# A 31-tap depthwise convolution as float32 diagonal products in four column groups of TensorE

## The chip, the cores and the metric

The kernel runs on one core of a Trainium2 chip, in one launch. The metric is the device time of that core in microseconds, the median over several runs. The engines are TensorE (PE in the profile, its weight loads PEld), VectorE (DVE), ScalarE (ACT), GpSimd (POOL) and SyncE (SP), which issues most of the DMAs.

## What is computed

Two transformer blocks work on 512 tokens of width 1024, all in float32. The first block has a parallel mixer, an attention to a memory of 256 tokens and a gated feed-forward part; the second has four gated feed-forward parts, a pooling mixer and a latent attention. The change touches the parallel mixer alone:

```python
def parallel_mixer(h, w_in, conv_dw, conv_dw_b, conv_ln_g, conv_ln_b, q_norm_g, k_norm_g, w_out, tabs):
    z = jnp.einsum("bsd,dc->bsc", h, w_in)
    ...
    a = a_val * jax.nn.sigmoid(a_gate)          # 512 channels, 512 tokens
    a = dwconv_centred(a, conv_dw, conv_dw_b)   # 31 taps a channel, zeros at both ends
    a = layernorm(a, conv_ln_g, conv_ln_b)      # over the 512 channels of a token
    a = jax.nn.silu(a)
    ...
    att = gqa_blocked(q, k, v)                  # 8 query heads of 64, 2 key heads
    mixed = jnp.concatenate([a, att], axis=-1)
    return jnp.einsum("bsc,cd->bsd", mixed, w_out)
```

## The kernel before

Activations lie with channels in the 128 partitions and the 512 tokens along the row. A float32 product is made exact by splitting both factors into a high part (type fp32r, made by a cast) and the low rest: `mm3` (L165) issues three TensorE matmuls, high x high, high x low and low x high. Weights come in units of 128 x 1024 words. `fetch` (L127) loads a unit into one of three `raw` buffers through SP's queue, and `cook` (L132) makes its high part on ScalarE (L138) and its low part on VectorE or GpSimd (L140); of the cooked parts there are three buffers each, too. `wshare` says how many of four units get their low part from GpSimd: all four in the mixer's input projection and in the memory's key and value projections (`W_IN, W_KV = 4, 4`), none in the output projection.

The mixer (L561) multiplies with `w_in` in 14 output tiles (`linear`, L172). Their order is `ORDER`: pairs of a gate and a value tile, which give the four channel tiles of the convolution, with k, v and four tiles of q between and behind them. `ev_gate` (L580) and `ev_val` (L597) turn a pair into the conv's input `at`, twice the gated value; half the conv's weights make up for it. Then come eight heads of attention, one head ahead: `scores` and `attend` (L682, L693), and after each head two units of the memory's projections (`mem_kv`, L464). The output projection multiplies attention's half first, then the conv's half.

The convolution of a channel tile is shared by two engines. `conv_pe` (L522) does six of the 31 taps on TensorE, as products with diagonal 128 x 128 matrices `dg` that GpSimd makes from the weights (L530), in exact parts: 18 matmuls for a tile into a PSUM tile `cps`, with shifts of whole pairs of words. `conv_taps` (L542) does the other taps: one on ScalarE (L548, with the bias), 24 on VectorE, each one instruction that multiplies a shifted row by its weight and adds (L556), and at last the sum with `cps` (L559). The taps are a generator that the mixer steps by hand: six taps behind each tile of the input projection, up to 30 before the attention and eight behind each head (`STEP_IN`, `STEP_PRE`, `STEP_HEAD`). `conv_norm` (L737) is the layernorm over the channels, also in steps, behind heads 3, 6 and 7; its mean is one float32 product of 512 columns (L745).

A float32 operand that isn't split goes to TensorE as it is. So do the sums of squares of the norms (`sums`, L202): float32 products with 32 output columns, one for each block of 128 tokens, whose four results go to the four groups of 32 partitions of one PSUM tile:

```python
for j in range(nb):
    self.nc.tensor.matmul(ps[32 * j:32 * j + 32, o:o + P], sel,
                          sq[:, j * P:(j + 1) * P], start=..., stop=...)
```

The order of the instructions on each engine is set when the kernel is built: a scheduler takes the program in its written order as priority, and lets ready instructions pass waiting ones by a model of their times. On the chip each queue then runs in that fixed order. Tiles come from pools with a fixed number of buffers; `xs` has 16 (the split input of the projection, then the attention's probabilities), `cv` nine (the conv), `pt` two in PSUM.

Of the kernel before, what the change touches and what calls it, by code (L numbers as in the profile page):

```python
# [26 lines left out]
# order of the taps' offsets: the even ones from the middle, then the odd ones  # L27
TAPS = sorted(range(-(KTAPS // 2), KTAPS // 2 + 1), key=lambda d: (d % 2, abs(d), d))
# [5 lines left out]
_VECS = [  # L34
    ("g_mix", 8), ("conv_w", 4 * KTAPS), ("conv_b", 4), ("cln_g", 4), ("cln_b", 4),
# [25 lines left out]
class Kern:  # L61
# [41 lines left out]
    # -- small access helpers --  # L103
# [7 lines left out]

    def t(self, tag="t", dt=F32, w=S, name="t"):
        return self.pools[tag].tile([P, w], dt, name=name, tag=tag)
# [7 lines left out]
    def turn(self, out, src):  # L121
        """Transpose by PE, which moves float32 words unchanged."""
        n = src.shape[0]
        return self.nc.tensor.transpose(out, src, self.ident[:n, :n])  # L124

    # -- weights: DRAM -> raw -> exact parts hi + lo --
# [17 lines left out]
    def lo_on_pool(self):  # L144
        """Share of the units (in fourths) whose low part GpSimd makes."""
        self.wturn = (self.wturn + 1) % 4
        return self.wturn < self.wshare
# [9 lines left out]
    def load_tile(self, w, nt, nk):  # L157
        """Stationary tiles of output tile nt: list over k of (hi, lo) [P, P]."""
        res = []
        for k0 in range(0, nk, 8):  # L160
            n = min(8, nk - k0)
            res += self.tiles(self.load_unit(w[nt, :, k0 * P:(k0 + n) * P], n * P), n)
        return res

    def mm3(self, ps, w, x, start, stop):  # L165
        """ps += w.T @ x with w, x each given as exact (hi, lo) parts."""
        mm = self.nc.tensor.matmul
        mm(ps, w[0], x[0], start=start, stop=False)  # L168
        mm(ps, w[0], x[1], start=False, stop=False)  # L169
        self.mmi = mm(ps, w[1], x[0], start=False, stop=stop)  # L170
# [10 lines left out]
    # -- split an fp32 tile (SBUF or PSUM), optionally scaled per partition --  # L181
# [31 lines left out]
    def columns(self, sm, dim, eps=0.0, w=1):  # L213
        """sm / dim + eps in columns [P, block, w], in PSUM."""
# [8 lines left out]
    def newton(self, v, n):  # L223
        """rsqrt of v [P, n] on the vector engine."""
# [14 lines left out]
    def rstd(self, sqs, dim, nb=4):  # L239
        """rsqrt(mean + eps) in columns from squares [P, nb * P], summed over the list."""  # L240
# [27 lines left out]
    def bcast_ps(self, R, nb=4, w=1):  # L268
        """Columns to rows of all partitions (row r of w in its share of them), exact float32."""
# [14 lines left out]
    def expand(self, R, w, tag="t"):  # L284
        """Columns -> [32 * block + r, tokens], zero outside the block, as exact parts."""
# [13 lines left out]
    def spread(self, X, r, tag="mi"):  # L299
        """Row r of every block, on all partitions."""  # L300
# [6 lines left out]
    # -- residual stream --  # L307
# [5 lines left out]
    def gather(self, sqs, sq, last, w=S):  # L313
        """Sum of squares so far: at most two tiles, the last one kept apart."""
# [6 lines left out]
    def pre(self, gname, dve_squares=(), tag2="xs"):  # L321
        """Gain times x as exact parts, and the reciprocal rms in quadrant form."""
# [14 lines left out]
    def post_collect(self, gname, tag="xs"):  # L337
        """Evacuation of a stage's output that a norm follows; pre() of the next stage adds it."""
# [10 lines left out]
    def settle(self):  # L349
        """Generator: adds the pending normed output to x, a tile a step."""  # L350
# [24 lines left out]
    def warm(self, ps, n):  # L375
        """Keeps PE's clock up while it waits: n products that nobody reads, right behind the
        last matmul."""
# [13 lines left out]
    # ------------------------------------------------------------------  # L391
    def softmax_rows(self, ps, w, f, tag):
        """softmax over ps[:, :w] * f (f: [P, 1], positive)."""
# [12 lines left out]
    def rope(self, src, g, gs, cos, sin):  # L406
        """Rotary embedding along the partitions (pairs 16 apart), gains g, gs folded in."""
# [11 lines left out]
    def stack(self, src, r, tag, on_pool=False):  # L419
        """Exact parts of the 64 rows src[64 r:], one in each half of a tile."""  # L420
# [8 lines left out]
    # -- block 1: parallel mixer --  # L429
    def mem_load(self, i):  # L430
        """Two 256-token tiles of the memory side by side."""
# [16 lines left out]
    def mem_prep(self):  # L448
        """Gain times memory as exact parts."""
# [14 lines left out]
    def mem_kv(self):  # L464
        """Generator: key and value projections of the memory, a weight unit a step."""
# [37 lines left out]
    NPE = 6  # L503
    PE_AT = 0
    CP_TAG = "pt"
    STEP_IN = 6
    KV_HEAD = 2
    STEP_PRE = 30
    STEP_HEAD = 8
    KT_TAG = "pr"  # L510
    PT_TAG = "t"
    CN_AT = (3, 6, 7)
    CN_AF = (0, 0, 1)
    ORDER = (0, 1, 8, 2, 3, 9, 4, 5, 10, 6, 7, 11, 12, 13)
    W_IN, W_KV, W_OUT, W_MEM = 4, 4, 0, 1

    def tap(self, n):
        """Output and input ranges of tap n."""
        d = TAPS[n]
        return (slice(0, S - d), slice(d, S)) if d >= 0 else (slice(-d, S), slice(0, S + d))  # L520

    def conv_pe(self, i, at):  # L522
        """The taps of channel tile i that run on PE, as products with diagonal matrices."""
        nc = self.nc
        ah, al = self.split(at, None, "cv", name="ah")
        ps = self.ps(self.CP_TAG, "cps")
        for n0 in range(0, self.NPE, 2):
            c = 2 * (i * KTAPS + n0)
            dg = self.t("pr", F32R, name="dg")
            nc.gpsimd.tensor_tensor(  # L530
                out=dg.rearrange("p (n t) -> p n t", n=4),
                in0=self.ident.unsqueeze(1).to_broadcast([P, 4, P]),
                in1=self.cws[:, c:c + 4].bitcast(F32).unsqueeze(2).to_broadcast([P, 4, P]),
                op=ALU.mult)
            for n in range(2):
                o, s = self.tap(n0 + n)
                hi, lo = dg[:, 2 * n * P:(2 * n + 1) * P], dg[:, (2 * n + 1) * P:(2 * n + 2) * P]
                self.mm3(ps[:, o], (hi, lo), (ah[:, s], al[:, s]), n0 + n == 0,
                         n0 + n == self.NPE - 1)
        return ps  # L540

    def conv_taps(self, i, at, acc):  # L542
        """Generator: the other taps of channel tile i, on DVE."""
        nc = self.nc
        w = lambda n: self.cwh[:, i * KTAPS + n:i * KTAPS + n + 1]
        first = KTAPS // 2
        o, sl = self.tap(first)
        nc.scalar.activation(acc[:, o], at[:, sl], AF.Identity, scale=w(first),  # L548
                             bias=self.v("conv_b", i))
        nc.gpsimd.tensor_copy(acc[:, :1], self.v("conv_b", i))  # L550
        ps = None
        for m, n in enumerate(n for n in range(self.NPE, KTAPS) if n != first):
            if m == self.PE_AT:
                ps = self.conv_pe(i, at)
            o, s = self.tap(n)
            nc.vector.scalar_tensor_tensor(out=acc[:, o], in0=at[:, s], scalar=w(n),  # L556
                                           in1=acc[:, o], op0=ALU.mult, op1=ALU.add)
            yield
        nc.vector.tensor_tensor(out=acc, in0=ps, in1=acc, op=ALU.add)  # L559

    def mixer(self):  # L561
        nc = self.nc
        a = self.a
        self.cwh = self.t("tb", name="cwh")[:, :4 * KTAPS]
        ws0 = {0: self.tiles(self.cook(self.raw0, UNIT, 4), 8)}
        xs, R1 = self.pre("g_mix", (1, 3, 5))
        nc.gpsimd.tensor_scalar(out=self.cwh, in0=self.v("conv_w", 0, 4 * KTAPS), scalar1=0.5,
                                scalar2=1.0, op0=ALU.mult, op1=ALU.mult)
        self.cws = self.t("tb", F32R, name="cws")[:, :8 * KTAPS]
        c2 = self.cws.rearrange("p (k two) -> p k two", two=2)  # L570
        nc.scalar.copy(c2[:, :, 0], self.cwh)
        nc.gpsimd.tensor_tensor(out=c2[:, :, 1], in0=self.cwh, in1=c2[:, :, 0].bitcast(F32),
                                op=ALU.subtract)
# [3 lines left out]
        # n-tiles: 0..7 (gate_i, val_i), 8 k, 9 v, 10..13 q pairs  # L577
        ats = []
# [7 lines left out]
        convs = []  # L586
        accs = []

        def step(n):
            while n and convs:  # L590
                try:
                    next(convs[0])
                    n -= 1
                except StopIteration:
                    convs.pop(0)

        def ev_val(nt, ps):  # L597
            i = nt // 2
            at = self.t("cv", name="at")
            acc0 = self.t("cv", name="acc0")  # L600
            nc.vector.tensor_tensor(out=at, in0=ps, in1=rb, op=ALU.mult)
            nc.vector.scalar_tensor_tensor(out=at, in0=st["g"], scalar=1.0, in1=at, op0=ALU.add,
                                           op1=ALU.mult)
            accs.append(acc0)
            convs.append(self.conv_taps(i, at, acc0))
# [3 lines left out]
        def ev_k(nt, ps):  # L609
# [6 lines left out]
            # both halves of a tile hold the same kv head  # L616
# [776 lines left out]
```

## Time and profile before

| | |
|---|---|
| median of 3 runs | 2589.59 us (2588.21 to 2589.89) |
| profiled execution | 2588.3 us from its first to its last instruction |
| TensorE busy | 2496.1 us (96%) |
| VectorE busy | 1385.5 us (54%) |
| ScalarE, GpSimd busy | 919.1 us (36%), 521.8 us (20%) |
| TensorE's mean granted clock | 0.985 of full |
| the mixer | about the first 322 us |

The profile is of one execution. A row of a group gives line, engine, operation, the tiles written and read, the shapes and the count, then busy time and mean duration, then the idle time of the engine just before and what ended it. A TensorE record lasts longer than the distance to the next one, since matmuls are pipelined: the distance between starts is the cost. The mean granted clock is taken over the whole span.

### The profile page before, as it was taken

Reading aid. Unit: us, or ns where it says so; the run is one execution under the profiler, and the core shown is the slowest. Engines: PE = TensorE matmul, PEld = TensorE weight load, DVE = VectorE, ACT = ScalarE, POOL = GpSimd, SP = SyncE. Lnnn points to the kernel's source line nnn. Section 1 sums busy time; section 2 is a strip of 40 time slices with the busy share of each in tenths; the row PEclk is TensorE's granted clock in tenths of the full one; section 3 lists DMA queues with packets and bytes.
Section 4 is the critical chain, followed back from the end, with each engine's and each line's share of the span. In section 5 each row is a group of like instructions: output and inputs, shape, how many; then the busy total and the mean of one; then the engine's idle time right before and its main releaser. Section 6 shows DMA issues by size and latency. Waiting matters only on the chain.

```text
span 2588.3 us, 29365 instructions
## 1 busy us (share of the span) xinstructions
PE 2496.1 (96%) x11668; PEld 2037.2 (79%) x11668; DVE 1385.5 (54%) x1877; ACT 919.1 (36%) x1332; POOL 521.8 (20%) x417
## 2 busy tenths in 40 slices
PE   7879989899999899999999999999999999999999
PEld 6667768688888688888888888888887778888887
DVE  7997563686632645533655543555433576555522
ACT  3336534354422333322422322323222455422221
POOL 4575232311100311101211100111000144111100
PEclk9889999999999999999999999999999999999999
DMA  4211211133333222234232333223332210333232
GB/s 163 66 67 49 90 57 58 64 98 98 96 95 97 69 94 96 95 98 132 74 98 98 97 98 96 97 95 95 98 98 88 78 62 19 104 98 97 92 107 79
DMA packets 68201, 229.80 MB, mean 89 GB/s; under 512 B 7456, under 2 KB 9632, under 8 KB 68064
## 3 DMA queue, kind: packets, MB, share of 16 engines
q1 hardware_dynamic: 66688, 225.35, 27.1%
q0 software_dynamic: 1232, 2.36, 0.3%
q8 instruction: 91, 1.49, 0.2%
q14 instruction: 46, 0.38, 0.0%
q10 hardware_dynamic: 144, 0.23, 0.0%
HBM read 225.80 MB, written 2.10 MB: 88 GB/s over the span
## 4 chain that ended last, share of the span: by engine, by line
PE 86%; DVE 4%; ACT 1%; issue 0%; ACTq 0%
PE ps L169 26%; PE ps L168 26%; PE ps L170 26%; DVE x L369 1%; DVE xl L190 1%; PE wo L168 1%; PE wo L169 1%; PE wo L170 1%; PE pt L124 1%; PE po L169 0%; PE bc L274 0%; PE po L168 0%; PE po L170 0%; PE sc L168 0%; DVE wlo L140 0%
## 5 line engine op out<-in xcount | busy, mean ns | idle before, releaser
L138 ACT CAST whi<-raw 128x1024 fp32r<-128x1024 f32 (+2 forms) x432 | 440.5, 1021 | 1217.7 <-PE ps L169 767.5
L140 DVE TENSOR_TENSOR wlo<-raw,whi 128x1024 fp32r<-128x1024 f32 (+2 forms) x400 | 559.3, 1400 | 492.6 <-ACT whi L138 487.5
L169 PE MATMUL ps<-xl,whi 128*128 128x512 f32 x2008 | 789.8, 394 | 18.6 <-DVE xl L190 18.5
L168 PE MATMUL ps<-xh,whi 128*128 128x512 f32 x2008 | 784.9, 393 | 15.0 <-ACT xh L189 14.7
L170 PE MATMUL ps<-xh,wlo 128*128 128x512 f32 x2008 | 786.6, 392 | 0.0
L169 PEld LDWEIGHTS ps<-xl,whi 128*128 128x128 f32 x2008 | 380.5, 189 | 104.6 <-DVE xl L190 25.0
L168 PEld LDWEIGHTS ps<-xh,whi 128*128 128x128 f32 x2008 | 379.7, 189 | 97.3 <-ACT xh L189 16.2
L170 PEld LDWEIGHTS ps<-xh,wlo 128*128 128x128 f32 x2008 | 380.7, 190 | 79.8 <-issue 0.9
L168 PE MATMUL ps<-ah,whi 128*128 128x512 f32 x880 | 342.3, 389 | 0.0
L169 PE MATMUL ps<-al,whi 128*128 128x512 f32 x880 | 342.3, 389 | 0.0
L170 PE MATMUL ps<-ah,wlo 128*128 128x512 f32 x880 | 342.3, 389 | 0.0
L877 DVE TENSOR_TENSOR g<-ps,bct 128x512 f32<-128x512 f32 x176 | 120.6, 691 | 389.9 <-PE ps L170 382.8
L882 POOL TENSOR_TENSOR g<-g 128x512 f32<-128x512 f32 x88 | 119.0, 1353 | 856.5 <-ACT whi L138 457.6
L317 POOL TENSOR_TENSOR sq<-sq 128x512 f32<-128x512 f32 x72 | 112.7, 1566 | 535.8 <-ACT sq L310 533.9
L170 PEld LDWEIGHTS ps<-ah,wlo 128*128 128x128 f32 x880 | 165.2, 188 | 34.4
L169 PEld LDWEIGHTS ps<-al,whi 128*128 128x128 f32 x880 | 165.2, 188 | 34.2
L168 PEld LDWEIGHTS ps<-ah,whi 128*128 128x128 f32 x880 | 165.2, 188 | 34.2
L556 DVE SCALAR_TENSOR_TENSOR acc<-at,cwh,acc 128x502 f32<-128x502 f32 (+12 forms) x96 | 114.1, 1201 | 1.0 <-ACT acc L548 0.5
L140 POOL TENSOR_TENSOR wlo<-raw,whi 128x1024 fp32r<-128x1024 f32 x32 | 81.3, 2542 | 71.4 <-ACT whi L138 71.2
L185 ACT CAST ah<-g 128x512 fp32r<-128x512 f32 x88 | 54.7, 622 | 112.8 <-POOL g L882 112.8
L387 DVE SCALAR_TENSOR_TENSOR x<-ps,x 128x512 f32<-128x512 f32 x40 | 27.5, 691 | 84.5 <-PE ps L170 84.4
L858 POOL TENSOR_TENSOR c<-c 128x512 f32<-128x512 f32 x22 | 29.7, 1348 | 208.3 <-DVE c L845 178.5
(298 smaller groups left out, 2594.8 us busy)
## 6 DMA issues: line engine op xcount, KB each, us to landing
raw<-in_wgu SPq DMA_DIRECT2D x176, 512.0 KB, 3.5
raw<-in_wd SPq DMA_DIRECT2D x64, 512.0 KB, 3.5
raw<-in_w_up SPq DMA_DIRECT2D x44, 512.0 KB, 3.5
raw<-in_wd SPq DMA_DIRECT2D x32, 384.0 KB, 3.1
raw<-in_w_down SPq DMA_DIRECT2D x16, 512.0 KB, 3.5
raw<-in_w_in SPq DMA_DIRECT2D x14, 512.0 KB, 4.0
raw<-in_mla_w_in SPq DMA_DIRECT2D x9, 512.0 KB, 3.5
raw<-in_mla_w_q SPq DMA_DIRECT2D x12, 384.0 KB, 3.0
```

The lines of the kernel that those rows point to most:

```text
L138: self.nc.scalar.copy(hi[:, s], raw[:, s])
L140: eng.tensor_tensor(out=lo[:, s], in0=raw[:, s], in1=hi[:, s].bitcast(F32), op=ALU.subtract)
L168: mm(ps, w[0], x[0], start=start, stop=False)
L169: mm(ps, w[0], x[1], start=False, stop=False)
L170: self.mmi = mm(ps, w[1], x[0], start=False, stop=stop)
L185: nc.scalar.copy(hi, src)
L317: self.nc.gpsimd.tensor_tensor(out=sqs[0][:, :w], in0=sqs[0][:, :w], in1=sq[:, :w], op=ALU.add)
L387: self.nc.vector.scalar_tensor_tensor(out=self.x[nt], in0=ps, scalar=scale, in1=self.x[nt], op0=ALU.mult, op1=ALU.add)
L556: nc.vector.scalar_tensor_tensor(out=acc[:, o], in0=at[:, s], scalar=w(n), in1=acc[:, o], op0=ALU.mult, op1=ALU.add)
L858: nc.gpsimd.tensor_tensor(out=c, in0=c, in1=st["g"], op=ALU.mult)
L877: nc.vector.tensor_tensor(out=g, in0=ps, in1=rb, op=ALU.mult)
L882: nc.gpsimd.tensor_tensor(out=g, in0=g, in1=st["g"], op=ALU.mult)
```

## The change

All 31 taps go to TensorE. `conv_in` makes a padded input of 544 words a row, with zeros at both ends, into which `ev_val` writes. `conv` loads ready-made diagonal weights of a channel tile (`conv_d`, one unit, not split), and copies each 32 channels of the input four times into one 128-partition tile `X[c]`, shifted by 0, 8, 16 and 24 words: 16 DMAs of 32 partitions on SP's queue. A float32 product with 128 rows and 32 output columns then adds four taps of 32 channels, and eight such steps (shifted by one word each) 32 taps, of which one has the weight zero. The four groups of 32 channels write to the four groups of 32 partitions of one PSUM tile, in turn. ScalarE takes the result out, halves it and adds the bias. `conv` is called behind head 0 for two tiles, behind heads 1 and 2 for one each, and the steps of `conv_norm` come behind heads 4, 5 and 6. VectorE's taps, GpSimd's diagonals, the packed conv weights and the splitting of the conv's input go away. In the mixer the low parts of the weights are all made on VectorE (`W_IN, W_KV = 0, 0`). The tiles of `xs` and `cv` grow to 520 and 544 words.

```diff
+HALO = KTAPS // 2
+SHIFTS, STEPS = 4, 8
...
+    WIDE = {"xs": S + STEPS, "cv": S + SHIFTS * STEPS}
     def t(self, tag="t", dt=F32, w=S, name="t"):
-        return self.pools[tag].tile([P, w], dt, name=name, tag=tag)
+        return self.pools[tag].tile([P, self.WIDE.get(tag, S)], dt, name=name, tag=tag)[:, :w]
...
-    CN_AT = (3, 6, 7)
-    CN_AF = (0, 0, 1)
+    CONV_AT = (0, 0, 1, 2)
+    CN_AT = (4, 5, 6)
...
-    W_IN, W_KV, W_OUT, W_MEM = 4, 4, 0, 1
+    W_IN, W_KV, W_OUT, W_MEM = 0, 0, 0, 1
...
-    def conv_pe(self, i, at):
...
-    def conv_taps(self, i, at, acc):
...
+    def conv_in(self):
+        xp = self.t("cv", w=self.WIDE["cv"], name="cp")
+        self.nc.gpsimd.memset(xp[:, :HALO], 0.0)
+        self.nc.gpsimd.memset(xp[:, HALO + S:], 0.0)
+        return xp
+
+    def conv(self, i, xp):
+        nc = self.nc
+        wd = self.fetch(self.a["conv_d"][i], UNIT)
+        W = S + STEPS - 1
+        X = []
+        for c in range(4):
+            t = self.t("xs", w=S + STEPS, name="cx")
+            for j in range(SHIFTS):
+                nc.sync.dma_start(out=t[32 * j:32 * j + 32, :W],
+                                  in_=xp[32 * c:32 * c + 32, STEPS * j:STEPS * j + W])
+            X.append(t)
+        ps = self.ps(self.CP_TAG, "cps")
+        for m in range(STEPS):
+            for c in range(4):
+                o = (4 * m + c) * 32
+                nc.tensor.matmul(ps[32 * c:32 * c + 32, :], wd[:, o:o + 32], X[c][:, m:m + S],
+                                 start=m == 0, stop=m == STEPS - 1)
+        acc = self.t("cv", name="acc")
+        nc.scalar.activation(acc, ps, AF.Identity, scale=0.5, bias=self.v("conv_b", i))
+        return acc
...
             nc.vector.tensor_tensor(out=at, in0=ps, in1=rb, op=ALU.mult)
-            nc.vector.scalar_tensor_tensor(out=at, in0=st["g"], scalar=1.0, in1=at, op0=ALU.add,
-                                           op1=ALU.mult)
-            accs.append(acc0)
-            convs.append(self.conv_taps(i, at, acc0))
+            xp = self.conv_in()
+            nc.vector.scalar_tensor_tensor(out=xp[:, HALO:HALO + S], in0=st["g"], scalar=1.0,
+                                           in1=at, op0=ALU.add, op1=ALU.mult)
+            xps.append(xp)
...
             attend(n)
-            with self.tc.issue_after(self.mxi.ins):
-                step(self.STEP_HEAD if n < self.CN_AT[0] else 1000)
+            for i in range(4):
+                if n == self.CONV_AT[i]:
+                    accs.append(self.conv(i, xps[i]))
             for _ in range(self.KV_HEAD):
                 next(self.kv)
-            for i in range(3):
-                if n == self.CN_AT[i]:
-                    with self.tc.issue_after((self.loi if self.CN_AF[i] else self.mxi).ins):
-                        next(cn)
+            if n in self.CN_AT:
+                next(cn)
...
+    w = f("conv_dw")[0].reshape(KTAPS, 4, 4, 32)
+    cd = np.zeros((4, SHIFTS, 32, STEPS, 4, 32), np.float32)
+    for d in range(KTAPS):
+        for c in range(32):
+            cd[:, d // STEPS, c, d % STEPS, :, c] = w[d, :, :, c]
+    out["conv_d"] = cd.reshape(4, P, UNIT)
```

## Rows read from the trace of the kernel before

**Rows 1.** Windows: stretch, length, busy (instructions) of PE, PEld, DVE, ACT, POOL; clock; DMA.

```profile
0.00:40.00 40.00, 31.93 (x189) 24.91 (x190) 23.02 (x44) 19.44 (x30) 17.94 (x17) 1.00 0.57 200
40.00:200.00 160.00, 123.76 (x618) 101.57 (x617) 157.13 (x208) 49.72 (x80) 101.48 (x62) 0.87 0.22 73
200.00:322.00 122.00, 116.98 (x575) 92.12 (x573) 76.60 (x155) 75.99 (x139) 45.54 (x41) 1.00 0.21 69
322.00:2588.00 2266.00, 2223.39 (x10290) 1818.57 (x10289) 1128.79 (x1472) 773.91 (x1085) 356.83 (x299) 0.99 0.28 89
```

**Rows 2.** Waits of PE to 325 us: total, times, longest.

```profile
PE ps L168 <- DVE mk L479: 9.9, 2, 7.7
PE ps L168 <- ACT xh L189: 7.4, 1, 7.4
PE bc L274 <- DVE y L235: 6.3, 1, 6.3
```

**Rows 3.** DVE groups of the mixer: count; busy us, mean ns; idle before.

```profile
L556 DVE SCALAR_TENSOR_TENSOR acc<-at,cwh,acc 128x502 f32<-128x502 f32 (+12 forms) x96 | 114.1, 1201 | 1.0 <-ACT acc L548 0.5
```

**Rows 4.** DVE in order of time, behind the last query: start, us.

```profile
151.13 0.28 DVE L217 TENSOR_SCALAR q<-qsum 128x128 f32<-128x128 f32 x1
...
151.66 7.35 DVE L556 SCALAR_TENSOR_TENSOR acc<-at,cwh,acc 128x501 f32<-128x501 f32 x4
...
169.66 0.19 DVE L261 SCALAR_TENSOR_TENSOR f<-y 128x32 f32<-128x32 f32 x1
```

**Rows 5.** PE in order of time, several stretches.

```profile
14.57 0.39 PE L170 MATMUL ps<-xh,wlo 128*128 128x512 f32 x1
...
63.76 2.85 PE L274 MATMUL bc<-con,f 128*64 128x128 f32 x16 [5.19 <-DVE f L261]
...
67.14 0.63 PE L168 MATMUL ps<-xh,whi 128*128 128x512 f32 x1
67.56 0.63 PE L169 MATMUL ps<-xl,whi 128*128 128x512 f32 x1
...
137.34 0.40 PE L170 MATMUL cps<-ahh,dg 128*128 128x510 f32 x1
137.57 0.39 PE L168 MATMUL cps<-ahh,dg 128*128 128x508 f32 x1
...
198.54 0.54 PE L170 MATMUL ps<-whi,ml 128*128 128x512 f32 x1
```

**Rows 6.** PE groups of the mixer, one of the conv's three alike.

```profile
L169 PE MATMUL cps<-ahl,dg 128*128 128x510 f32 (+3 forms) x24 | 10.2, 425 | 4.4 <-DVE ahl L187 4.4
```

**Rows 7.** PE in order of time, the mean over the conv channels.

```profile
235.56 1.12 PE L745 MATMUL mean<-tot,con 128*128 128x512 f32 x2 [0.75 <-DVE tot L743]
```

**Rows 8.** PE in order of time, sums of squares.

```profile
15.12 1.74 PE L208 MATMUL sum<-sq,con 128*32 128x128 f32 x56
16.79 0.50 PE L169 MATMUL ps<-xl,whi 128*128 128x512 f32 x1
```

**Rows 9.** POOL groups of the mixer.

```profile
L140 POOL TENSOR_TENSOR wlo<-raw,whi 128x1024 fp32r<-128x1024 f32 x28 | 71.7, 2564 | 46.4 <-ACT whi L138 46.2
```

**Rows 10.** DVE group of the weights' low parts, whole kernel (page, part 5).

```profile
L140 DVE TENSOR_TENSOR wlo<-raw,whi 128x1024 fp32r<-128x1024 f32 (+2 forms) x400 | 559.3, 1400 | 492.6 <-ACT whi L138 487.5
```

**Rows 11.** Window of the later attention stage, columns as in the first group.

```profile
2030.00:2320.00 290.00, 283.69 (x1488) 228.01 (x1486) 180.60 (x351) 136.26 (x249) 78.48 (x91) 0.98 0.21 69
```

**Rows 12.** DMA issues on SP's queue in order of time.

```profile
1.19 5.02 SPq L94 DMA_DIRECT2D x<-in_xT  x8
...
7.30 0.33 SPq L661 DMA_DIRECT2D cos<-in_rope  x1
```

**Rows 13.** DMA issues of the whole kernel: count, KB each, us to landing.

```profile
x<-in_xT SPq DMA_DIRECT2D x8, 256.0 KB, 5.1
...
outT<-x SPq DMA_DIRECT2D x8, 256.0 KB, 2.0
```

**Rows 14.** PEld groups from 15 to 17 us.

```profile
L208 PEld LDWEIGHTS sum<-sq,con 128*32 128x32 f32 x56 | 1.5, 110 | 0.4 <-issue 0.4
```

More of the change, by code (lines that the diff above doesn't have):

```diff
@@ L26 @@
 KTAPS = 31
-TAPS = sorted(range(-(KTAPS // 2), KTAPS // 2 + 1), key=lambda d: (d % 2, abs(d), d))
+HALO = KTAPS // 2
+SHIFTS, STEPS = 4, 8
 UNIT = 1024
@@ L34 @@
 _VECS = [
-    ("g_mix", 8), ("conv_w", 4 * KTAPS), ("conv_b", 4), ("cln_g", 4), ("cln_b", 4),
+    ("g_mix", 8), ("conv_b", 4), ("cln_g", 4), ("cln_b", 4),
     ("gq", 1), ("gqs", 1), ("gk", 1), ("gks", 1), ("g_mixpost", 8), ("g_mempre", 8),
@@ L501, in mem_kv @@
             yield
-    NPE = 6
-    PE_AT = 0
     CP_TAG = "pt"
-    STEP_IN = 6
     KV_HEAD = 2
-    STEP_PRE = 30
-    STEP_HEAD = 8
     KT_TAG = "pr"
     PT_TAG = "t"
-    CN_AT = (3, 6, 7)
-    CN_AF = (0, 0, 1)
+    CONV_AT = (0, 0, 1, 2)
+    CN_AT = (4, 5, 6)
     ORDER = (0, 1, 8, 2, 3, 9, 4, 5, 10, 6, 7, 11, 12, 13)
-    W_IN, W_KV, W_OUT, W_MEM = 4, 4, 0, 1
-    def tap(self, n):
-        d = TAPS[n]
-        return (slice(0, S - d), slice(d, S)) if d >= 0 else (slice(-d, S), slice(0, S + d))
@@ L522, in conv_pe @@
-    def conv_pe(self, i, at):
-        nc = self.nc
-        ah, al = self.split(at, None, "cv", name="ah")
-        ps = self.ps(self.CP_TAG, "cps")
[L527 to L540, printed above, removed]
@@ L542, in conv_taps @@
-    def conv_taps(self, i, at, acc):
[L544 to L559, printed above, removed]
+    W_IN, W_KV, W_OUT, W_MEM = 0, 0, 0, 1
@@ L563, in mixer @@
         a = self.a
-        self.cwh = self.t("tb", name="cwh")[:, :4 * KTAPS]
         ws0 = {0: self.tiles(self.cook(self.raw0, UNIT, 4), 8)}
         xs, R1 = self.pre("g_mix", (1, 3, 5))
[L567 to L573, printed above, removed]
         cos, sin = self.t("tb", name="cos1"), self.t("tb", name="sin1")
@@ L576, in mixer @@
         st = {}
-        ats = []
         def ev_gate(nt, ps):
@@ L584, in ev_gate @@
             st["g"] = g
[L586 to L595, printed above, removed]
+        xps, accs = [], []
         def ev_val(nt, ps):
-            i = nt // 2
-            at = self.t("cv", name="at")
-            acc0 = self.t("cv", name="acc0")
+            at = self.t(name="at")
             nc.vector.tensor_tensor(out=at, in0=ps, in1=rb, op=ALU.mult)
-            nc.vector.scalar_tensor_tensor(out=at, in0=st["g"], scalar=1.0, in1=at, op0=ALU.add,
-                                           op1=ALU.mult)
-            accs.append(acc0)
-            convs.append(self.conv_taps(i, at, acc0))
+            xp = self.conv_in()
+            nc.vector.scalar_tensor_tensor(out=xp[:, HALO:HALO + S], in0=st["g"], scalar=1.0,
+                                           in1=at, op0=ALU.add, op1=ALU.mult)
+            xps.append(xp)
         ks, vh = [], []
@@ L667, in mixer @@
                 self.mem_prep()
-            step(self.STEP_IN)
         fcol = self.inner_rstd(qsum[:, :P], 64, R1, 8, post=64.0 ** -0.5)
         self.wshare = self.W_KV
-        after = self.last.ins
         self.kv = self.mem_kv()
-        with self.tc.issue_after(after):
-            step(self.STEP_PRE)
         mix = []
@@ L1294, in host_arrays @@
         "g_mix": _cols(f("norm_mix_pre")[0]),
-        "conv_w": f("conv_dw")[0][np.array(TAPS) + KTAPS // 2].T.reshape(4, P, KTAPS).transpose(1, 0, 2).reshape(P, -1),
         "conv_b": _cols(f("conv_dw_b")[0]), "cln_g": _cols(f("conv_ln_g")[0]),
```

## The prediction

> **What bounds the kernel now.** I read first the busy time by engine in four stretches, the mixer cut in three [rows 1]. TensorE is busy 2223 of the 2266 us after the mixer, which the change leaves alone, so all there is to win lies in the first 322 us. In the mixer the middle stretch stands out: from 40 to 200 us TensorE works 123.8 of 160 us, at a mean granted clock of 0.87, while VectorE is busy 157.1. Before it TensorE loses 8 us, 7.4 of them until the first tile of x is there, and after it, from 200 us on, 5.0 of 122.
>
> The waits of TensorE come second [rows 2]: apart from the start, the long ones are for VectorE results (mk, y and others of 4 to 5 us). So VectorE ends last in that stretch. Why it is late stands in the groups of VectorE [rows 3]: 96 taps at 1.20 us, 114.1 us in all. An example in order of time [rows 4]: the chain that turns qsum into the scores' factor starts at 151.1 and ends at 169.9, though its first and last step take 0.28 and 0.19 us; between them stand taps, four of them 7.35 us in a row.
>
> The third loss is the clock [rows 5]. Behind each stop of some microseconds the granted clock is at the lower of its two levels (1.2 instead of 2.4 GHz): matmuls of 512 columns start 0.43 us apart, and later 0.23. There are seven such stretches between 63.8 and 198.9 us, 31 us together, which at the full rate would be half as long: 15.7 us lost. The one at the start (7.4 to 14.6 us) costs 3.6 more and stays.
>
> So TensorE's work in the mixer at the full clock is 322 - 49.3 idle (322 less the 31.9, 123.8 and 117.0 of [rows 1]) - 15.7 - 3.6 = 253.4 us.
>
> **The change part by part.** *TensorE, removed:* 4 tiles x 6 taps x 3 products = 72 matmuls [rows 6], 0.23 us apart [rows 5]: 16.6 us.
>
> *TensorE, added:* 4 tiles x 32 float32 products with 32 output columns each. Of such a product the trace has two records: the mean over the channels is one product of 512 columns, two records, 1.12 us [rows 7]. A record outlives the start of its successor by 0.16 us (0.39 long, 0.23 apart [rows 5]), so each takes 0.48 us. That makes 256 records, 123 us, if they run one after another. Whether the column groups run side by side is seen in the sums of squares, which have the same form (float32, 128 rows, 32 columns, four column groups in turn) with a quarter of the columns: 56 records from 15.12 to 16.79 [rows 8], 1.67 us, 29.8 ns each. One after another they would need 56 x 0.12 = 6.7 us, four times that. So a record of 512 columns costs 0.12 us in such a run, and the four tiles 256 x 0.12 = 30 us. The switches between the forms at both ends of that run are inside its 1.67 us. I take 30 us; the other bound is the 123.
>
> The Trainium skill, TensorE: Matmul & The Clock Gate, Part 3 (Packing small matmuls), has three column tiles of 512 columns speed up by 2.38, not 3; four at that rate give about 3.2, an estimate from that page, and the 123 us would become 39. The trace's factor of four is the nearer evidence, as its products are float32 and of this form.
>
> Half of the new products start at an odd word of their row; every tap that TensorE ran before was even, so no row shows what an odd start costs: between nothing and double time for 128 of 256 records, 15 us. I take nothing, since records of 510 and 508 columns, which start or end off the tile's edge too, last 0.39 us like those of 512 [rows 5], and keep the 15 for the range.
>
> *VectorE:* it loses the 96 taps, 114.1 us [rows 3] (and eight operations of tiles, which I leave uncounted), and gets the low part of 28 weight units (the 28 of GpSimd [rows 9]) at the 1.40 us of that operation over the whole kernel [rows 10], 39.2. Its 256.7 us in the mixer (23.0, 157.1 and 76.6 [rows 1]) become 182, 63% of some 288. That is the load of the later attention stage (180.6 of 290 us, 62%, weight low parts included), where TensorE is idle 6.3 us in 290 [rows 11]. So VectorE no longer ends last, and its short chains follow each other as after 200 us. *GpSimd* loses these 71.7 us [rows 9] and the diagonal matrices, which costs and gives nothing by itself; the shorter units (1.40 instead of 2.56) only lessen the wait for a raw buffer. *ScalarE* trades four casts and four first taps for four evacuations, hidden behind TensorE, since ScalarE works 145 of the 322 us (19.4, 49.7 and 76.0 [rows 1]). If that cover were gone it would be 4 x 0.8 us.
>
> *SyncE's queue:* 4 fetches and 64 shifted copies. An issue takes 0.33 to 0.63 us [rows 12], so the 16 of a tile take 5 to 10 us, and behind them on the same queue wait the fetches of the memory's weights. The copies of tiles 0 and 1 want buffers of the xs pool, which the input projection holds until its last tile; the conv weights, used as they come, hold one raw buffer of three for each tile until the products have run. So at the entry into the attention two tiles want 10 to 20 us of the queue, and the weight units behind them have one raw buffer. The cover is TensorE's own work: cooked units in three buffers (24 matmuls of 256 columns each for the keys, half of 0.23 us: 2.8 us a unit), two heads' scores, and tile 0's products (7.7 us) while tile 1 loads. Landing has no row from one place on the chip to another; the nearest are 2.0 us (output) and 5.1 (x) [rows 13]. I put 3 us of stop here. Without the cover it is about 20, as a rival below.
>
> *The sum:* start 11.0 (7.4 and 3.6), work 253.4 - 16.6 + 30 = 266.8, stops 10: the 5.0 that the last stretch has now, 3 at the entry, 2 elsewhere by the 2% of the later attention stage. 287.8 instead of 322, 34 us less. The profiled execution lasted 2588.3 us, 1.3 below the median of the runs: 2554 on its scale, 2555.5 on theirs; I say 2555.
>
> **The rivals.** *The column groups don't run side by side* (another order of the queue, or a wait between products into one bank). Then the conv costs up to 123 us, +93: 2648. It decides from 64 us (0.25 us a record) upwards; two abreast (61 us) end at 2586, no change. For it: these records are four times as long as those of the sums, and other products may be put between them. Against it: the 56 records.
>
> *Weight loads that don't hide.* Each record has a load of its own, 0.11 us [rows 14]. If a load waited for the product before it on the same rows, the 256 records would stand in line with their loads: 256 x 0.59 = 151 us, +121: 2676. The 29.8 ns between records, shorter than one load, speaks against it. The Trainium skill's same page, Part 3, says that loads overlap with running products only when the row groups differ; here all use all rows, and by the trace that doesn't hold.
>
> *The copies are late.* The two tiles' 32 issues and their landing aren't covered: 2 x (10 + 5) = 30 us less the work at hand, about 20, and the lower clock behind each stop: +20 to 25, 2575 to 2580, still a gain. For it: one queue, pools shared with the weights. Against it: TensorE has work there that waits for none of it.
>
> *Nothing won, since VectorE stays last:* for it only that 39 us of low parts come to it; its 63% speaks against. It would need 100 us more than counted, and I give it no chance of its own.
>
> **How the numbers follow.** My forecast (2543 to 2570; the lower end is a mixer with no stop beyond the start and 28 us for the conv, the upper the 15 us of odd starts): 0.74. Late copies (2570 to 2590): 0.15. Groups in line or in pairs (2586 to 2650): 0.09, loads in line 0.02. 2540 to 2586 leaves out the last two, some of the third and a rest of the first. A change of 0.2%, 5 us, is about what this kernel's times can tell from none. Faster: 0.74 and most of the late copies, 0.87; same 0.03; slower 0.10.
>
> **What would show it.** Right: in the stretch 40 to 200 TensorE near 97% busy and the clock at 1.00; conv records in runs of 64 that take 7 to 8 us; no tap on VectorE and its load near 180 us; first weights of the memory's queries fetched some 30 us sooner. Wrong: a conv run of 15 us or more, or one cut up by other products; TensorE waiting for the copies; a VectorE still full from 40 to 200 us.

## The result, and the profile after

The changed kernel takes 2616.14 us (median of 4 runs, 2615.53 to 2617.2); beside it the kernel before took 2588.9. The ratio is 1.0105, 95% interval 1.0091 to 1.012: 27 us slower, where I had forecast 34 us faster. The profiled execution took 2615.53 us, its span is 2613.8, against 2588.3 before.

Windows of the changed kernel; columns and stretches as in [rows 1], the mixer's end moved from 322 to 303 us:

```profile
0.00:40.00 40.00, 32.55 (x195) 25.25 (x196) 23.23 (x47) 18.03 (x27) 4.50 (x19) 1.00 0.58 202
40.00:200.00 160.00, 152.37 (x930) 105.73 (x930) 88.10 (x184) 70.19 (x126) 43.08 (x42) 0.98 0.38 115
200.00:303.00 103.00, 95.11 (x445) 73.96 (x447) 54.85 (x99) 55.09 (x92) 20.78 (x19) 0.98 0.24 77
303.00:2613.00 2310.00, 2267.03 (x10289) 1820.47 (x10289) 1127.01 (x1472) 772.82 (x1084) 356.18 (x299) 0.99 0.28 87
```

The mixer did what it was to do: from 40 to 200 us TensorE works 152.4 of 160 us at a clock of 0.98 (123.8 at 0.87 before), and VectorE has fallen from 157.1 to 88.1. The loss is in the last row. Behind the mixer TensorE ran 10290 instructions before and runs 10289 now, as good as the same; they kept it busy for 2223.4 us, and now for 2267.0. That is 43.6 us in code that the diff doesn't touch, at the same clock of 0.99.

To part the two, a mark: the first sums of squares behind the mixer, TensorE in order of time. Before:

```profile
322.08 0.43 PE L208 MATMUL sum<-sq,con 128*32 128x128 f32 x8
```

After:

```profile
302.93 0.42 PE L211 MATMUL sum<-sq,con 128*32 128x128 f32 x8
```

Up to the mark the kernel is 19.2 us shorter, from the mark to the end of the span 44.7 us longer (2613.8 - 302.9 = 2310.9, against 2588.3 - 322.1 = 2266.2). The difference, 25.5, is that of the two spans. The work behind the mark repeats closely: it takes 2266.2 us in the other kernels below that keep the old offsets and the old mixer, while the mark itself lies anywhere from 320.1 to 322.1 us where the mixer is that of before.

How the work behind the mark grew is seen where TensorE has nothing but split products of 512 columns. One such stretch, 300 us of the first feed-forward stage, before and after:

```profile
520.00:820.00 300.00, 300.00 (x1325) 248.48 (x1324) 168.68 (x202) 118.71 (x153) 35.74 (x26) 1.00 0.31 96
```

```profile
520.00:820.00 300.00, 300.00 (x1294) 242.81 (x1293) 152.82 (x182) 111.06 (x142) 33.94 (x25) 1.00 0.31 95
```

TensorE is busy all the time at the full clock in both, and does 1325 products in one and 1294 in the other. (As records overlap, one more stands in a window than starts in it: 300 / 1324 is 226.6 ns from start to start, 300 / 1293 is 232.0.) In the trace some 8920 of these products follow each other directly behind the mixer; 4.9 ns on each is 43.7 us. The slower products are there from 15 us on, before the new convolution has run, and their spacings, some 225 to 240 ns, come back in the same order later in the same stage. That points to where the operands lie, not to a state that something leaves behind. The groups of the feed-forward's second products (duration min/median/max) show the spread; before and after:

```profile
L168 PE MATMUL ps<-ah,whi x880: 389/389/389, 721.5 to 2583.4; 128*128 128x512 f32 x176
```

```profile
L171 PE MATMUL ps<-ah,whi x880: 388/393/404, 709.2 to 2608.8; 128*128 128x512 f32 x176
```

**Where the tiles lie.** A split product reads two operands: a moving tile (a row of 512 words that streams through) and a weight slice (the 128 columns of one product, 512 bytes of a unit). All buffers of a pool follow each other in every partition. Before, each was 512 words, 2048 bytes, and a weight unit 4096, so every such moving tile started at a multiple of 256 bytes (of 512 too) from the weight slices. The diff's `WIDE` gives xs 520 words (2080 = 8 x 256 + 32 bytes) and cv 544 (2176 = 8 x 256 + 128). So each tile of xs starts 32 bytes further off than the one before it, those of cv 0 or 128, and all those of the pools behind them (pr, m, q, t, tb) 128, since 16 x 32 + 9 x 128 bytes are 6 x 256 + 128. Besides, the packed vectors lost 124 columns, which moved everything by 512 bytes.

**The theories.** Theory 1: the place of a moving tile, relative to the weight slices, makes the split products slower. Theory 2: the shift of the whole layout by 512 bytes does. Theory 3: something that the new mixer does or leaves behind slows TensorE.

### The profile page after: what moved, and what is told of

Same layout as the page of the kernel before. It is cut to its first block, busy times and chain, and to the rows that moved or that the text cites. A ratio compares the mean times of both kernels' runs of the same rounds, so it can differ in the third digit from the quotient of the medians.

```text
span 2613.8 us, 29753 instructions
## 1 busy us (share of the span) xinstructions
PE 2547.1 (97%) x11852; PEld 2025.4 (77%) x11852; DVE 1293.2 (49%) x1801; ACT 916.1 (35%) x1327; POOL 424.5 (16%) x379
## 4 chain that ended last, share of the span: by engine, by line
PE 94%; DVE 4%; ACT 1%; issue 0%; DMA 0%; ACTq 0%; DVEq 0%
PE ps L172 28%; PE ps L171 28%; PE ps L173 28%; PE cps L539 1%; DVE x L372 1%; PE pt L127 1%; DVE xl L193 1%; PE wo L171 1%; PE po L172 1%; PE wo L172 1%; PE wo L173 1%; PE po L171 1%; PE po L173 1%; PE bc L277 1%; PE sum L211 0%
## 5 line engine op out<-in xcount | busy, mean ns | idle before, releaser
L143 DVE TENSOR_TENSOR wlo<-raw,whi 128x1024 fp32r<-128x1024 f32 (+2 forms) x428 | 591.6, 1384 | 531.9 <-ACT whi L141 525.8
L173 PEld LDWEIGHTS ps<-ah,wlo 128*128 128x128 f32 x880 | 165.6, 188 | 38.7
L193 DVE SCALAR_TENSOR_TENSOR xl<-x,vec,xh 128x512 fp32r<-128x512 f32 x72 | 68.4, 974 | 0.1
L190 DVE TENSOR_TENSOR al<-g,ah 128x512 fp32r<-128x512 f32 x88 | 63.0, 718 | 8.0 <-ACT ah L188 7.7
L403 ACT ACTIVATE p<-sc,nb,f 128x512 f32<-128x512 f32 (+3 forms) x80 | 53.6, 675 | 36.3 <-DVE nb L401 35.4
```

The costliest lines, as they stand in the source:

```text
L143: eng.tensor_tensor(out=lo[:, s], in0=raw[:, s], in1=hi[:, s].bitcast(F32), op=ALU.subtract)
L190: self.loi = eng.tensor_tensor(out=lo, in0=src, in1=hi.bitcast(F32), op=ALU.subtract)
L193: nc.vector.scalar_tensor_tensor(out=lo, in0=src, scalar=scale, in1=hi.bitcast(F32), op0=ALU.mult, op1=ALU.subtract)
L403: nc.scalar.activation(p[:, :w], ps[:, :w], AF.Exp, bias=nb, scale=f, accum_out=l)
```

## The experiments

**The wide buffers alone, in the kernel before.**

```
+    WIDE = {"xs": S + 8, "cv": S + 32}
...
-        return self.pools[tag].tile([P, w], dt, name=name, tag=tag)
+        return self.pools[tag].tile([P, self.WIDE.get(tag, S)], dt, name=name, tag=tag)[:, :w]
```

> The kernel before, with nothing changed but the size of the buffers in two pools (520 words for each of the 16 of xs, 544 for each of the 9 of cv, where all had 512). Theory 1, the place of the operands in SBUF: the split matmuls of 512 columns start 0.232 us apart instead of 0.227 in every stage, some 8650 of them, so about 45 us more: 2630 to 2636. Theory 2 (the whole layout sits 512 bytes lower in the changed kernel) and theory 3 (the work of the new mixer slows TensorE later): no change, 2589, and 0.227 us.

Measured: 2633.92 us, ratio 1.0175 (1.0159 to 1.019). No product, copy or engine is changed, and the kernel is 45 us slower; the window of 520 to 820 us holds 1294 products, as in the changed kernel:

```profile
520.00:820.00 300.00, 300.00 (x1294) 242.77 (x1294) 166.52 (x201) 117.28 (x152) 34.05 (x25) 1.00 0.31 95
```

Theory 3 falls for these 45 us, and so does theory 2, as the vectors kept their size.

**The 512 bytes.**

```
-    ("gkn", 1), ("gkp", 1), ("gkps", 1), ("f2g0", 8), ("f2g1", 8),
+    ("gkn", 1), ("gkp", 1), ("gkps", 1), ("f2g0", 8), ("f2g1", 8), ("pad", 4 * KTAPS),
```

> The changed kernel with 124 unused columns put back into the packed vectors, so that every buffer sits 512 bytes higher, as it did before. Theory 2: the split matmuls go back to 0.227 us and the time to some 2571. Theory 1 and theory 3: 2616, no change.

Measured: 2620.79 us, ratio 1.0123 (1.0106 to 1.014), 1294 products in that window. Theory 2 is out. It is 5 us above the changed kernel, and none of that is in the spacing of the split products: 0.8 us are there at the mark, and the rest arises between 2150 and 2206 us, in the latent attention, where the order in which TensorE's instructions were laid down differs between the two kernels. There TensorE waits 3.9 us for VectorE's `ol` at a clock of 0.97; the changed kernel waits 0.3 us in that stretch. Elsewhere behind the mark the two keep step within 0.3 us. By this a rebuilt order can move the kernel by 5 us; it is not shown by a run of its own.

**The changed kernel with buffers of 512 words.** The products make 505 columns; VectorE makes the last seven.

```
-    WIDE = {"xs": S + STEPS, "cv": S + SHIFTS * STEPS}
...
+            nc.gpsimd.memset(t[:64, :HALO], 0.0)
+            nc.gpsimd.memset(t[64:, S - STEPS - 1:], 0.0)
...
+        for s in range(R):
+            nc.vector.tensor_tensor(out=pr[:, s * KTAPS:(s + 1) * KTAPS], in0=e[:, s:s + KTAPS],
+                                    in1=self.v("conv_w", i * KTAPS, KTAPS), op=ALU.mult)
```

> The changed kernel with all buffers of xs and cv at 512 words again: the products make 505 columns of a tile, zeros at the edges are set in the copies' tiles, and the last seven columns come from VectorE (seven small products and one sum a tile). Theory 1: all split matmuls at 0.227 us, 45 us less than the changed kernel, some 2571, and so below the kernel before by 15 to 20. Theory 2: half way at most, since the layout is that of before here too, so it gives the same 2571 and only the run with the 512 bytes parts the two. Theory 3: 2616, matmuls at 0.232.

Measured: 2576.59 us, ratio 0.9953 (0.9938 to 0.9968): 40 us below the changed kernel, 12 below the one before. Its window:

```profile
520.00:820.00 300.00, 300.00 (x1325) 248.43 (x1324) 158.11 (x189) 114.25 (x146) 33.96 (x25) 1.00 0.32 97
```

1325 products again. Behind the mark (308.94 us here) it takes 2266.0 us, what the kernel before takes. The mixer itself is 6 us longer than the changed kernel's: TensorE waits 2.4 us for shifted copies, and on GpSimd the zeros of the third tile wait 6.5 us (until 139.6 us; the profile puts it down to the copies), with the probabilities' last step behind them in the same queue.

**Which offsets cost.** Four kernels with unused bytes ahead of some pools, one run of each. The edit, here for 64 and 64 bytes:

```
+    PAD = {'xs': 16, 'pr': 16}
...
+            if n in self.PAD:
+                pp = E(tc.tile_pool(name=n + "_pad", bufs=1))
+                pad = pp.tile([P, self.PAD[n]], F32, name=n + "pad")
...
+            self.pools[n] = E(tc.tile_pool(name=n + "_pool", bufs=b))
```

> The kernel before, all buffers at 512 words, with 64 unused bytes ahead of the pools of xs and cv and 64 more ahead of pr, m, q and those after them. The moving tiles so lie 64 and 128 bytes off the step of the weight slices. Theory 1, if any such offset costs: 0.232 us in the products with tiles from xs and in those with tiles from m and q, some 2633. If only the step from buffer to buffer costs, not the offset: 2589. Theories 2 and 3: 2589.

> The kernel before with 256 unused bytes ahead of the pools of xs and cv and 256 more ahead of pr, m, q and those after them, so that the moving tiles lie 256 and 512 bytes off the place they had. Theory 1a, what counts is the offset from the step of 512 bytes in which the weight slices follow each other: products with tiles from xs 0.229 to 0.232 us apart, those with tiles from m and q 0.227 as before, time some 2605 to 2615. Theory 1b, every change of place costs, also by 512: 0.232 in both and 2618 as with 64 and 128 bytes.

Measured: 2617.64 us with 64 and 128 bytes, 2588.05 with 256 and 512. Windows of the first (from 540 us on the moving tiles are from xs; from 740 us 9 of 44 are from cv, the others from pr, m and q):

```profile
540.00:700.00 160.00, 160.00 (x701) 131.28 (x700) 108.22 (x134) 68.88 (x89) 19.61 (x16) 1.00 0.31 96
740.00:820.00 80.00, 80.00 (x347) 64.94 (x346) 18.00 (x16) 21.37 (x28) 7.52 (x5) 1.00 0.33 96
```

and of the second:

```profile
540.00:700.00 160.00, 160.00 (x707) 132.52 (x706) 108.59 (x135) 70.34 (x90) 19.37 (x15) 1.00 0.30 98
740.00:820.00 80.00, 80.00 (x355) 66.26 (x354) 18.27 (x16) 20.99 (x26) 7.49 (x5) 1.00 0.32 97
```

At 64 bytes a product takes 160 / 700 = 228.6 ns, with 35 of 44 tiles at 128 bytes 80 / 346 = 231.2; at 256 and at 512 the windows hold 707 and 355, the same as in the kernel before. So it isn't the step from buffer to buffer (2048 bytes in all of these), and not any change of place: offsets of 256 and 512 bytes are free. My theory 1a had put 256 among those that cost. At 64 bytes a product costs less than the 0.232 us that I had expected for any offset, so the time is 2618 and not 2633.

> The kernel before with 128 unused bytes ahead of everything, so that weights and moving tiles move together and keep their offset to each other. If the offset between the moving tile and the weight slices is what costs: 0.227 us apart and 2588, no change. If each tile's own place counts (which 64 and 128 bytes changed, and 256 and 512 did not): 0.232 us and some 2630.

The edit is a tile of 32 words ahead of all others. Measured: 2589.08 us, no change:

```profile
520.00:820.00 300.00, 300.00 (x1325) 248.40 (x1324) 167.61 (x200) 117.67 (x151) 35.74 (x26) 1.00 0.31 96
```

An offset of 128 bytes between the operands costs, the same 128 bytes under both don't. So it isn't a tile's own place that counts, but its offset from the weights.

> The changed kernel with 128 unused bytes between the pools cv and pr, and nothing else: the tiles of pr, m, q, t and tb then lie at a multiple of 256 bytes from the weights, those of xs and cv, with their wide buffers, as in the changed kernel. If the offset of each tile counts by itself: the products with tiles from m and q go from 0.232 to 0.227 us, those with tiles from xs and cv stay at 0.232; a third of some 8650 products, 14 to 18 us less, 2598 to 2602. If the wide buffers alone cost, wherever the others lie: 2616, no change.

Measured: 2600.02 us, with 128 bytes of padding as the only edit of the changed kernel. Its windows, the first with tiles from xs (691 in the changed kernel too), the second with tiles from cv, pr, m and q (346 there):

```profile
540.00:700.00 160.00, 160.00 (x691) 129.30 (x690) 104.39 (x130) 67.78 (x87) 18.02 (x14) 1.00 0.29 92
740.00:820.00 80.00, 80.00 (x354) 66.09 (x353) 17.51 (x16) 21.15 (x26) 8.52 (x6) 1.00 0.33 97
```

The group of its second feed-forward products has 389 ns as its median again. The spread that is left is that of the 9 of 44 tiles that lie in cv: of the 22 channel tiles that an output tile sums over, the products with the first three start 230 ns apart, and those with the eighth to the next to last 226.7.

```profile
L176 PE MATMUL ps<-ah,whi x880: 387/389/398, 708.0 to 2593.3; 128*128 128x512 f32 x176
```

**The order of the convolution's products.**

```
-        for m in range(STEPS):
-            for c in range(4):
+        for c in range(4):
+            for m in range(STEPS):
```

> The changed kernel with its two loops over the products exchanged: all eight of one column group, then the eight of the next, so that the same 32 output columns follow each other. If the four column groups run side by side only when they come in turn, the 64 records of a tile take four times as long, 30 us instead of 7.6, and the kernel some 90 us longer: 2705. If records of one column group overlap as well: 2616, no change.

Measured, in one run: 2677.72 us, 62 more than the changed kernel. TensorE in order of time, first the changed kernel, then this one:

```profile
125.38 7.92 PE L539 MATMUL cps<-cx,raw 128*32 128x512 f32 x68
133.23 0.50 PE L648 MATMUL sc<-kh,st 128*128 128x512 f32 x1
133.57 0.40 PE L649 MATMUL sc<-kl,st 128*128 128x512 f32 x1
133.90 1.05 PE L539 MATMUL cps<-cx,raw 128*32 128x512 f32 x2
134.87 0.50 PE L648 MATMUL sc<-kh,st 128*128 128x512 f32 x1
```

```profile
154.03 17.42 PE L539 MATMUL cps<-cx,raw 128*32 128x512 f32 x48
171.38 0.50 PE L648 MATMUL sc<-kh,st 128*128 128x512 f32 x1
```

(A float32 product leaves two records, so a column group of a tile has 16 and a tile 64.) In turn, 68 records take 7.9 us, 116 ns each; group by group 48 take 17.4, 361 ns each. The column groups run side by side in the order of the change. Added up over the ten runs of records, from the first start to the start of the next other product, the convolution takes 33.9 us; here it takes 93.9.

Both averages hold more than the records themselves. Where the run in the other order has one column group alone, its 16 records take 6.99 us, 437 ns each:

```profile
224.33 7.06 PE L539 MATMUL cps<-cx,raw 128*32 128x512 f32 x16
231.32 0.66 PE L127 MATMUL pt<-con,p 128*128 128x128 f32 x4
```

Inside such a run the starts are 429 ns apart. The average over 48 is lower because the records overlap for a stretch where one group's end and the next group's begin. In the changed kernel's order, eight records (a product of each of the four groups) start every 0.86 us inside a run: 107 ns a record, a quarter of 429. So the four groups run fully side by side, and the ends of a run make the 116. A record in line costs 0.43 us and not the 0.48 that I had reckoned, and with the overlap the loss was 62 us and not 90.

The rows show one thing more: a pair of records between other products costs 0.97 us (133.90 to 134.87). Four records, of two products, cost the same in the changed kernel, and eight, of four products, in the kernel with 512 words:

```profile
154.31 1.05 PE L539 MATMUL cps<-cx,raw 128*32 128x512 f32 x4
155.29 0.50 PE L172 MATMUL po<-ptl,vh 128*128 128x512 f32 x1
```

```profile
160.06 1.05 PE L545 MATMUL cps<-cx,raw 128*32 128x505 f32 x8
161.05 0.50 PE L171 MATMUL po<-ptl,vh 128*128 128x512 f32 x1
```

So a lone pair is dear because nothing runs beside it: 0.86 us are its two records in line. The switch itself costs less: 0.11 us of the 0.97, and 0.2 in the two full-width products between the runs above, which take 0.34 and 0.33 us (133.23 to 133.90) where 0.23 is usual.

**Tile 0 ahead of the scores.**

```
+        accs.append(self.conv(0, xps[0]))
         scores(0)
...
-            for i in range(4):
+            for i in range(1, 4):
```

> The changed kernel with the products of channel tile 0 issued ahead of the first scores, where TensorE stands still for 6.5 us and then runs at the lower clock. If that stop only wants work (my forecast put its 3 us there): the 7.6 us of products fill it, 6 to 9 us less, some 2608 to 2611. If the copies can't be there yet, since they want buffers of the input projection: no gain, 2616, and a wait for a DMA in the stop's place.

Measured: 2614.01 us, ratio 1.0098 (1.0082 to 1.0113): 2 below the changed kernel, hardly to be told from none by the times; the mark comes 2.8 us sooner (300.13). What it was to fill, in the changed kernel, TensorE in order of time:

```profile
112.65 0.80 PE L648 MATMUL sc<-kh,st 128*128 128x512 f32 x1 [6.46 <-ACT p L403]
...
113.67 0.63 PE L648 MATMUL sc<-kh,st 128*128 128x512 f32 x1
114.10 0.63 PE L649 MATMUL sc<-kl,st 128*128 128x512 f32 x1
```

and the same place in this run:

```profile
100.05 1.05 PE L539 MATMUL cps<-cx,raw 128*32 128x512 f32 x2
...
109.11 7.06 PE L539 MATMUL cps<-cx,raw 128*32 128x512 f32 x58
116.10 0.50 PE L648 MATMUL sc<-kh,st 128*128 128x512 f32 x1
...
119.23 0.50 PE L648 MATMUL sc<-kh,st 128*128 128x512 f32 x1 [1.50 <-ACT p L403]
```

The stop has gone from 6.5 to 1.5 us, and the clock of 80 to 125 us has risen from 0.92 to 0.95; no wait for a DMA is there. But the convolution now runs in 15 pieces and takes 38.7 us, 4.8 more. Neither expectation came true: the stop could be filled, and most of what that gave went into lone pairs, of which there are ten here and four in the changed kernel.

**The edges on VectorE.** The products make columns 15 to 495 from unpadded copies; a sliding window on VectorE makes the other 31, and tile 0 goes first.

```
+        N = S - KTAPS
...
+            win = bass.AP(tensor=v.tensor, offset=v.offset, ap=[list(v.ap[0]), [1, b], [1, KTAPS]])
+            nc.vector.tensor_tensor(out=pr, in0=win, in1=wb, op=ALU.mult)
+            nc.vector.tensor_reduce(out=r[:, HALO * h:HALO * h + b], in_=pr,
+                                    axis=mybir.AxisListType.X, op=ALU.add)
```

> All buffers of xs and cv at 512 words, the products making columns 15 to 495 alone, which need no zeros and copies of 488 columns; the 31 columns at the edges come from VectorE (two products with a sliding window and two sums a tile), and tile 0 goes ahead of the first scores. Theory 1: 0.227 us everywhere; against the run with 512 words it saves its 4 us of waits for copies and zeros, and the stop ahead of the scores, 6 to 9 us: 2563 to 2568. If VectorE's added work (about 4 us a tile) delays the short chains: 2572 to 2577, no gain over the run with 512 words.

> The version with the edges on VectorE, tile 0 where the changed kernel has it, behind the first scores. It parts the two edits of that version: against the run with 512 words it shows the zeros and the late copies alone (4 us less, 2572, if they were what delayed TensorE there), and the rest of the 9.5 us between the two is tile 0's place. If tile 0's place is worth only the 2 us that it was worth in the changed kernel: 2569.

Measured: 2567.13 us, ratio 0.9918 (0.9901 to 0.9934), and 2571.35, 0.9932 (0.9915 to 0.9948), with tile 0 in its old place. So the edges alone give 5.2 us against the run with 512 words, tile 0's place 4.2; in the traces both lie ahead of the mark (308.9, 303.9 and 297.1 us). The first is the fastest version here, 22 us below the kernel before and 49 below the changed one.

**The low parts on GpSimd again**, in that version.

```
-    W_IN, W_KV, W_OUT, W_MEM = 0, 0, 0, 1
+    W_IN, W_KV, W_OUT, W_MEM = 4, 4, 0, 1
```

> The version with the edges on VectorE and tile 0 first, but with the low parts of the 28 weight units on GpSimd again, as they were before. My forecast's step: where VectorE is under two thirds busy and GpSimd free, it makes no difference who does them, 2565 to 2569. The rival: GpSimd takes 2.56 us a unit and not 1.40, the weights come later and TensorE waits for them, 5 us or more longer: 2572 and up. If VectorE's short chains (scores' factor, parts of the probabilities) gain by having less ahead of them: 3 us or more shorter, below 2564.

Measured: 2572.08 us, ratio 0.9935 (0.992 to 0.995), 5 us longer. Windows with the low parts on VectorE, then on GpSimd:

```profile
80.00:125.00 45.00, 43.12 (x263) 29.07 (x262) 28.44 (x64) 19.79 (x40) 21.95 (x22) 1.00 0.29 89
```

```profile
80.00:125.00 45.00, 41.76 (x237) 27.48 (x235) 25.69 (x54) 19.75 (x39) 31.46 (x26) 0.92 0.28 83
```

TensorE loses 1.4 us more to waits at the entry into the attention, and 8% of the clock, which is some 3.6 us of these 45 by the two levels. So in this version this part of the change is worth 5 us; the mark comes at 303.0 us instead of 297.1. Whether GpSimd's slower units or its lost time for other work brings the waits, the run doesn't part.

## Why the prediction was wrong

**The step that failed** is the sentence on which the whole sum was built: "TensorE is busy 2223 of the 2266 us after the mixer, which the change leaves alone". The change left the code alone and moved the operands. I took the wider buffers for a matter of space and gave them no term, no bound and no rival. Their price is 43.6 us behind the mixer, shown by the wide buffers alone (+45), by taking them away (-40, while the mixer lost 6) and by 128 bytes of padding (-16). With that term the forecast would have been 2599, on the slower side. Without that price the change would have stood at some 2571 (2616.1 less the 44.7 behind the mark), 17 us faster and not 34, and still above my range: the mixer's terms were off too, by 15 us.

The Trainium skill, SBUF — State Buffer, under Who interferes with whom, gives TensorE two independent read ports, one for moving rows and one for weight loads, and says that it never waits on anyone. By that, no offset between the two would cost anything. The runs here differ: 226.6 ns at multiples of 256 bytes, 228.6 at 64, 231.2 mostly at 128. The loads themselves last as long in both kernels (242.81 us for 1293, 248.48 for 1324: 188 ns each). What in the chip makes it so, no run shows.

**The mixer** came out as 302.9 us and not 287.8, by these terms:

- *TensorE's work.* The windows hold 280.0 us of busy time up to 303; less the lower clock (3.6 at the start, as before, and some 5 later) it is 271, against 266.8 in the sum. The convolution took 33.9 us and not 30: full runs go at 116 to 120 ns a record, as the sums of squares had said [rows 8], and the lone pairs at 0.97 us come on top. That the runs would be cut up by other products I had named as a sign of being wrong, but the sum had no term for it. The 624 products of the projections cost 2.4 more by their operands' place. Odd starts cost nothing that can be seen: the eight steps of a tile, odd and even, follow each other 0.86 us apart.
- *The stops.* I had put 10 us; 15.5 were idle and some 5 lost to the lower clock. The entry into the attention took 6.5 us, and 3.6 by the clock (0.92 in 80 to 125 us), where I had 3. But it is a wait for the scores' factor and the probabilities, not for the copies that I had put there: TensorE waited for none of them.
- *VectorE* did stop being last, as forecast, with 166 us of work up to 303 us (182 forecast); a wait of 3.1 us for parts of the probabilities at 219.5 us is the longest that it causes between 125 us and the mark.

**The rivals.** *Groups that don't run side by side*: not in the change's order; the other order shows that the mechanism is real and that a tile's 64 records then take 23 us. The gain of the four groups inside a run, 429 against 107 ns, is the 4 that I took from 56 short records. The Trainium skill, TensorE: Matmul & The Clock Gate, Part 3 (Packing small matmuls), from whose 2.38 for three I had estimated 3.2, has less; averaged over whole runs with their ends, 361 against 116 ns is 3.1. My price for the groups in line, 123 us, was too high: in the other order they took 93.9. *Loads that don't hide*: inside a run the records follow each other in 107 ns and each load lasts 109, so they hide. *Late copies*: didn't happen in the changed kernel. The rival that won wasn't among them.

**GpSimd's relief**, which I had called worth nothing by itself, is worth 5 us in the version where it was tried, in the waits and the clock at the entry. No run shows it for the changed kernel itself.

## What to carry to other kernels

When a change alters the size of a buffer, look at where every later buffer ends up: keep tiles that TensorE streams at a multiple of 256 bytes from the weight slices, with padding or by making tiles of odd width fit. A diff's reach is not the lines it touches; compare the start-to-start time of the commonest instruction in a stretch where its engine is always busy, before and after, as a first look. And where products of narrow column groups are to run side by side, put the groups in turn, keep their runs whole, and where a run must be broken, break it behind a full set of groups: one product alone takes as long as four side by side.

## What the runs showed of the hardware

- A split product (128 rows, 128 columns of weights, 512 moving columns) starts 226.6 ns after the one before when the moving tile's offset from the weight slices is a multiple of 256 bytes (the layout of before, and that moved by 256 and by 512), 228.6 at 64, 231.2 mostly at 128, and 232.0 in the changed kernel, where the offsets go in steps of 32 bytes. Moving weights and tiles together by 128 bytes changes nothing.
- Records of float32 products (128 rows, 32 output columns, 512 moving columns) start 429 ns apart when they are of one column group, and eight every 0.86 us, 107 ns each, when four column groups come in turn.
- Two, four or eight such records, of one, two or four column groups, between other products cost 0.97 to 0.99 us. The Trainium skill, TensorEngine Tiling (Array Packing), under Tiling Modes, has a change of the mode drain the engine. The rows fit that: some 0.3 us go with an interruption beyond the 0.86 of a product, 0.11 in the pair and 0.2 in the products beside it. That a drain is the reason, no run shows.
